# Output projection, second norm and expert search in two token halves, with one gather stream for u and v rows

## The chip, the cores and the metric

One core of a Trainium2 chip. The metric is device microseconds of one launch, the median of the runs. Engines are named as in the profile: PE is TensorE's matmuls (PEld its weight loads), DVE is VectorE, ACT ScalarE, POOL GpSimd, SP SyncE. Each engine works through its own instructions in order and waits on semaphores for the others.

## The reference, cut to what matters

One transformer layer over 512 latent tokens of width 2048, in float32:

```python
h = modulate(rms_norm(x, g_norm1), sh1, sc1)
q, k, v, bg, cg, u = split_proj(h @ w_in)          # 8 attention heads of 128, 1024 conv channels
o_attn = neighbourhood_attention(q, k, v, kc, vc, rpb)   # also sees 256 context tokens
o_conv = short_conv(u, bg, cg, w_conv)
y = concatenate([group_rms(o_attn), group_rms(o_conv)]) @ w_out
x = x + gt1 * y
h2 = modulate(rms_norm(x, g_norm2), sh2, sc2)
x = x + gt2 * peer(h2, w_pq, sub_keys, u_experts, v_experts)
```

`sh`, `sc` and `gt` come from `silu(c) @ w_ada + b_ada`, 12288 columns. `peer` chooses for each token, in each of 8 heads, 16 of 16384 experts: a query of two halves is scored against 128 keys each, the 16 best of either side are combined, and the 16 best sums win. For its 128 experts a token then computes

```python
act = gelu(einsum('nd,ned->ne', h2, u_tab[expert])) * gate
out = einsum('ne,ned->nd', act, v_tab[expert])
```

## The kernel before, in words

All activations lie transposed, features on the 128 partitions and tokens along the free axis. A weight tile is 128 x 1024 float32 (512 KB). `weights` (lines 93 to 100) loads it through a ring of four raw buffers on SP's queue, rounds it to `hi` on ACT and subtracts to `lo` on DVE, with four buffers each. Every product is then three matmuls, hi by hi, hi by lo and lo by hi (`mm3`, lines 102 to 105), so a tile of eight 128 x 128 blocks gives 24 matmuls.

The stages in order of time:

- Modulation, first half (before 136 us), then attention, one head after the other (`project`, `qk_norm`, `attention`, `out_norm`), to about 600 us.
- Convolution channels, eight groups of three projections, to 873 us. The second part of the modulation runs beside it: `ada_tasks` (line 261) is a generator, and each step loads one tile of `w_ada` through the same raw ring and multiplies and adds it on DVE (lines 293 and 295). A chunk of 1024 columns takes 16 steps, then `row_sums` and `columns_of` collect it through PE. Six of the eight chunks lie here, twelve steps a group, and two in the output projection.
- Output projection (lines 443 to 462): 16 output parts `m`, each 2 weight tiles and 48 matmuls of 512 tokens, evicted by DVE into `R` with gate and residual, stored to `x1d`, squared and summed.
- Second norm (lines 464 to 478): `rstd_of`, then for each of 16 feature blocks three operations on DVE and one on ACT that write the normalised tokens to `HH` and `HL` as hi and lo.
- Query and search (lines 533 to 650): 16 queries of 48 matmuls of 512 tokens. `half_top` takes the 16 best of 128 scores for each of four blocks of 128 tokens on DVE, `head_top` combines two of them; POOL and ACT then find the experts' numbers (lines 595, 603 to 605), and `hit_sums` reduces them on DVE. A step's parts are put one or two queries later, so that other work lies between. Six u blocks run beside the last head.
- u stage: 128 `u_block`s (line 515), each 2 weight tiles and 48 matmuls, for the first 352 tokens against all experts; gelu on ACT, stored to `gu`. Beside it `one_hots` and `scatter` build each token's gate values per expert by small matmuls and store them to `gd`.
- v stage (lines 846 to 882): 16 groups `g` of 8 column steps `dq`, each 2 weight tiles and 48 matmuls of 352 tokens. `prepare` loads a group's share of `gd` and `gu`, multiplies and splits them one group ahead; DVE adds the results into `acc`, and `finish` writes the output in the last group.

The last 160 tokens (`NG`) are not multiplied with all experts. Their rows are gathered: `gather` (line 715) issues an indirect DMA on POOL's queue that brings one row of 2048 per partition (1 MB), 160 of them from `u` and 160 from `v`, with two row buffers. A u row is multiplied with h2 and summed on DVE (line 737), a v row is scaled and added on DVE (line 745), and a buffer's next fetch goes out when its use is over. The two streams are spread by `paced`: 161 steps over the 121 u blocks that follow the search, and 161 steps over the first 120 column steps of v.

The framework plans each engine's order at build time from the program's order and its own costs; `issue_after` pins an instruction behind another (the gather's uses behind the latest weight split).

## Time and profile before

| | us |
|---|---|
| median of 3 runs | 3448.43 |
| lowest and highest | 3443.44, 3456.69 |
| the profiled execution | 3443.56 |
| its span | 3441.8 |

In the span PE is busy 3287.1 us (96%), PEld 3019.0, DVE 2492.6, ACT 1177.3 and POOL 670.8. The DMA engines moved 912.52 MB, 265 GB/s on the mean. Matmuls are pipelined: the duration of one is longer than the distance to the next, and so a busy share of 96% is not yet PE at its peak. What a matmul costs is read from the distance of two starts. A wait counts only where PE stands behind it in the end.

### The profile page before, as it was taken

The page shows a single profiled execution, that of the slowest core. Times are in us where ns is not written, and L with a number is a line of the kernel's source. Part 1 is how long each engine was busy: PE and PEld are TensorE (multiplying, and loading weights), DVE is VectorE, ACT ScalarE, POOL GpSimd, SP SyncE. Part 2 cuts the span into 40 slices and gives each one's busy share as a digit, 9 for nine tenths or more (in the row PEclk, how much of TensorE's full clock was granted, in tenths as well). Part 3 has the DMA queues.
Part 4 walks back from the last instruction along what each step waited for, and adds up shares of the span by engine and source line. Part 5 has one row for each costly group of instructions (what it writes and reads, how often), then busy time and mean ns, then how long its engine had stood idle before and what let it go on. Part 6 is the DMA issues. An engine that isn't in the chain of part 4 may idle for free.

```text
span 3441.8 us, 48157 instructions
## 1 busy us (share of the span) xinstructions
PE 3287.1 (96%) x18951; PEld 3019.0 (88%) x18951; DVE 2492.6 (72%) x3648; ACT 1177.3 (34%) x1582; POOL 670.8 (19%) x402
## 2 busy tenths in 40 slices
PE   5899999999999988999999999999989989989999
PEld 1488888878887878999999999999989989989999
DVE  4444444888756888787888887676787887878885
ACT  3344444222324454333333333333222222322222
POOL 0000000000001663222211222222323223322320
PEclk9999999999999999999999999999999999999999
DMA  8722222888772226999999999998898998989986
GB/s 303 234 67 63 66 66 61 289 278 286 242 237 85 86 83 229 334 341 336 339 343 337 328 339 340 355 360 303 319 344 316 343 343 322 353 328 336 338 323 210
DMA packets 265316, 912.52 MB, mean 265 GB/s; under 512 B 23809, under 2 KB 77313, under 8 KB 222721
## 3 DMA queue, kind: packets, MB, share of 16 engines
q1 hardware_dynamic: 208208, 527.74, 44.6%
q0 software_dynamic: 46080, 335.56, 25.7%
q10 hardware_dynamic: 10800, 46.14, 3.4%
q8 instruction: 149, 2.44, 0.3%
q14 instruction: 79, 0.64, 0.1%
HBM read 854.82 MB, written 54.53 MB: 264 GB/s over the span
## 4 chain that ended last, share of the span: by engine, by line
PE 63%; DMA 19%; DVE 10%; issue 4%; POOL 2%; ACT 1%; SPq 0%; DVEq 0%; ACTq 0%; POOLq 0%
DMA row<-v,exi 11%; PE sps L105 8%; PE sps L103 8%; PE sps L104 8%; PE xps L103 4%; PE xps L105 4%; PE xps L104 4%; DVE accg L745 3%; DMA raw<-wada 3%; DVE wlo L99 3%; PE ops L105 3%; PE ops L103 2%; PE ops L104 2%; DMA row<-u,exi 2%; PE gps L709 2%
## 5 line engine op out<-in xcount | busy, mean ns | idle before, releaser
L98 ACT ACTIVATE whi<-raw 128x1024 fp32r<-128x1024 f32 x672 | 709.2, 1058 | 1642.6 <-PE sps L104 442.1
L99 DVE TENSOR_TENSOR wlo<-raw,whi 128x1024 fp32r<-128x1024 f32 x664 | 810.2, 1237 | 283.4 <-ACT whi L98 253.6
L105 PE MATMUL sps<-HH,wlo 128*128 128x352 f32 x2048 | 665.4, 325 | 21.4 <-DVE wlo L99 21.4
L103 PE MATMUL sps<-HH,whi 128*128 128x352 f32 x2048 | 671.8, 328 | 1.1 <-ACT whi L98 1.1
L104 PE MATMUL sps<-HL,whi 128*128 128x352 f32 x2048 | 663.7, 324 | 0.0
L105 PE MATMUL ops<-Ah,wlo 128*128 128x352 f32 x1536 | 505.4, 330 | 54.1 <-DVE wlo L99 54.0
L103 PE MATMUL ops<-Ah,whi 128*128 128x352 f32 x1536 | 503.2, 328 | 5.6 <-DVE acc L877 5.6
L104 PE MATMUL ops<-Al,whi 128*128 128x352 f32 x1536 | 499.5, 325 | 0.0
L745 DVE SCALAR_TENSOR_TENSOR accg<-row,dots,accg 128x2048 f32<-128x2048 f32 x160 | 375.6, 2348 | 160.1 <-DMA row<-v,exi 160.1
L723 POOL DMA_INDIRECT row<-v,exi x160 | 300.5, 1878 | 697.0 <-DVE accg L745 672.6
L105 PEld LDWEIGHTS sps<-HH,wlo 128*128 128x128 f32 x2048 | 387.9, 189 | 24.3 <-DVE wlo L99 24.3
L103 PEld LDWEIGHTS sps<-HH,whi 128*128 128x128 f32 x2048 | 388.3, 190 | 1.4 <-ACT whi L98 1.4
L104 PEld LDWEIGHTS sps<-HL,whi 128*128 128x128 f32 x2048 | 388.3, 190 | 0.0
L723 POOL DMA_INDIRECT row<-u,exi x160 | 226.1, 1413 | 785.1 <-DVE row L737 690.8
L105 PEld LDWEIGHTS ops<-Ah,wlo 128*128 128x128 f32 x1536 | 295.5, 192 | 61.1 <-DVE wlo L99 61.1
L737 DVE SCALAR_TENSOR_TENSOR row<-row,h2row 128x2048 f32<-128x2048 f32 x128 | 291.5, 2287 | 64.9 <-DMA row<-u,exi 64.7
L103 PE MATMUL xps<-HH,whi 128*128 128x512 f32 x768 | 306.0, 398 | 2.0 <-ACT whi L98 2.0
L105 PE MATMUL xps<-HH,wlo 128*128 128x512 f32 x768 | 303.6, 395 | 0.5 <-DVE wlo L99 0.5
L104 PE MATMUL xps<-HL,whi 128*128 128x512 f32 x768 | 303.2, 395 | 0.0
L103 PEld LDWEIGHTS ops<-Ah,whi 128*128 128x128 f32 x1536 | 293.9, 191 | 6.9 <-issue 4.1
L104 PEld LDWEIGHTS ops<-Al,whi 128*128 128x128 f32 x1536 | 294.7, 192 | 0.0
L99 POOL TENSOR_TENSOR wlo<-raw,whi 128x1024 fp32r<-128x1024 f32 x8 | 20.0, 2496 | 1003.4 <-ACT whi L98 1003.4
(274 smaller groups left out, 4943.0 us busy)
## 6 DMA issues: line engine op xcount, KB each, us to landing
raw<-uT SPq DMA_DIRECT2D x256, 512.0 KB
raw<-vb SPq DMA_DIRECT2D x256, 512.0 KB
raw<-wada SPq DMA_DIRECT2D x192, 512.0 KB
raw<-win SPq DMA_DIRECT2D x96, 512.0 KB
gu<-ug ACTq DMA_DIRECT2D x64, 352.0 KB
gd<-stg ACTq DMA_DIRECT2D x11, 2048.0 KB
gt<-gd SPq DMA_DIRECT2D x32, 704.0 KB
gl<-gu SPq DMA_DIRECT2D x32, 704.0 KB
```

What stands on the lines that cost most here:

```text
L98: weights.hi = nc.scalar.activation(hi, raw, AF.Copy)
L99: weights.lo = (eng or nc.vector).tensor_tensor(lo, raw, hi.bitcast(F32), op=ALU.subtract)
L103: nc.tensor.matmul(ps, lw[0], rw[0], start=start, stop=False)
L104: nc.tensor.matmul(ps, lw[0], rw[1], start=False, stop=False)
L105: return nc.tensor.matmul(ps, lw[1], rw[0], start=False, stop=stop)
L709: nc.tensor.matmul(gps[:, j, :], oj[:, j, :], oi[:, j, :], start=True, stop=True)
L723: nc.gpsimd.indirect_dma_start(out=row.rearrange("p k d -> p (k d)"), out_offset=None, in_=ap[tab], in_offset=bass.IndirectOffsetOnAxis(ap ...
L737: nc.vector.scalar_tensor_tensor(row, row, 1.0, h2row if s < P else h2ext, op0=ALU.mult, op1=ALU.mult, accum_out=dots[:, s:s + 1])
L745: nc.vector.scalar_tensor_tensor(ag, row, dots[:, s:s + 1], ag, op0=ALU.mult, op1=ALU.add)
```

## The change

The modulation sums move: four of the eight chunks go into the attention heads (4, 5 and 5 steps after the three projections of a head, their sums in `R`'s free tiles), the other four into the convolution (9 steps a group where there were 12). None is left in the output projection.

The output projection, the second norm and the search are done for tokens 256 to 511 first, then for tokens 0 to 255. Weights of `w_out` and `w_pq` are loaded and split for each half, and their matmuls have 256 columns instead of 512. The order is: output parts of the second half; two parts of the first half; norm of the second half; search of the second half with the other fourteen output parts of the first half between its queries (`between_a`), the norm of the first half at its query 14, and five u blocks at its end; `gathered`; search of the first half with 42 u blocks between its queries (`between_b`); the other 81 u blocks; v. The POOL variant of the weight split in `query` goes.

The gather is one stream, 160 u rows and then 160 v rows in the same two buffers, 321 steps over 251 units: half a unit for each query of the second search, one for each u block after the first five and for each of the 120 column steps. The v accumulators are `h2row` and `h2ext` themselves, written first by a scaling, so the two zeroed tiles and their memsets go. The scatter's generator now takes two steps at every fourth u block. Pools change sides, and PSUM banks are dealt anew.

```diff
-BANKS = {... "query": (0, 1, 2), ... "gps": (0, 1, 2), "tp": (3,), "u": (4, 5, 6), ...
+H = T // 2
+TL = 2
+BANKS = {... "query": (2, 5), ... "gps": (0, 2, 5), "tp": (3,), "u": (4, 6, 1), ...
...
+        tasks = ada_tasks(range(4), lambda c: R[:, 4 + 2 * (c % 2):6 + 2 * (c % 2), :].rearrange("p a t -> p (a t)"),
+                          iter((r_tile(3, "rows"), r_tile(5, "rows"))).__next__)
         for hd in range(NH):
             qps, _ = project(3 * hd, False)
+            run_tasks(tasks, 4)
...
             kps, kcps = project(3 * hd + 1, True)
+            run_tasks(tasks, 5)
...
             vps, vcps = project(3 * hd + 2, True)
+            run_tasks(tasks, 5)
...
-        tasks = ada_tasks(cnv, range(0, 6))
+        tasks = ada_tasks(range(4, 8), lambda c: cnv.tile([P, 1024], F32, tag="ada", bufs=2, name="ada"),
+                          lambda: cnv.tile([P, 512], F32, tag="rows", name="rows"))
...
-            run_tasks(tasks, 4)
+            run_tasks(tasks, 3)
...
+    def out_part(m, half):
+        cols = slice(H * half, H * half + H)
+        xm = op.tile([P, H], F32, tag="xm", bufs=4, name="xm")
+        nc.sync.dma_start(xm, ap["xT"][:, m, cols])
+        ps = psum("proj", "yps", P, H)
+        for hf in range(2):
+            w = weights(ap["wout"][m, hf])
+            for k in range(8):
+                kk = 8 * hf + k
+                mm3(ps, (w[0][:, k, :], w[1][:, k, :]), (y2[kk][0][:, cols], y2[kk][1][:, cols]), kk == 0, kk == KD - 1)
+        return m, half, ps, xm
+
+    def out_evict(m, half, ps, xm):
+        cols = slice(H * half, H * half + H)
+        xo = X[:, m, :]
+        nc.vector.scalar_tensor_tensor(xo, ps, mod2[:, m:m + 1], xm, op0=ALU.mult, op1=ALU.add)
+        nc.sync.dma_start(x1d[m][:, cols], xo)
...
+    for m in range(KD):
+        out_evict(*out_part(m, 1))
...
+    early = [out_part(m, 0) for m in range(2)]
+    norm2(1)
...
-    def query(c):
-        ps = psum("query", "qps", P, T)
+    def query(c, half):
+        cols = slice(H * half, H * half + H)
+        ps = psum("query", "qps", P, H)
         for hf in range(2):
-            w = weights(ap["wpq"][c, hf], nc.gpsimd if c % 2 == 1 and hf == 0 else None)
+            w = weights(ap["wpq"][c, hf])
...
+    def search(half, qs, between):
...
+        for c in range(1, 2 * NH + 4):
+            nxt = None
+            if c < 2 * NH:
+                nxt = query(c, half)
+            between(c)
...
+    def gather():
+        rows = []
+        todo = [("u", s) for s in range(NS)] + [("v", s) for s in range(NS)]
...
+        for n, (tab, s) in enumerate(todo):
+            with tc.issue_after(mark["dve"].ins):
+                (use_u if tab == "u" else use_v)(s, rows[n])
+            fetch()
+            yield
...
+    def use_v(s, row):
+        ag = accg[0 if s < P else 1]
+        if s in (0, P):
+            nc.vector.tensor_scalar(ag, row, dots[:, s:s + 1], None, op0=ALU.mult)
         else:
+            nc.vector.scalar_tensor_tensor(ag, row, dots[:, s:s + 1], ag, op0=ALU.mult, op1=ALU.add)
...
+    def between_a(c):
+        if c <= 12:
+            out_evict(*out_part(c + 1, 0))
+        elif c == 13:
+            for m in (14, 15):
+                out_evict(*out_part(m, 0))
+        elif c == 14:
+            norm2(0)
+            ops_.close()
+            u_block.pool = us.enter_context(pool("uo", side="right", **reuse))
+        elif c >= 16:
             u_block()
+            if c == 17:
+                u_block()
+
+    qs = query(0, 1)
+    gather_rows()
+    for x in early:
+        out_evict(*x)
+    us = ExitStack()
+    search(1, qs, between_a)
...
+    gathered()
+    accg = [h2row, h2ext]
+    NGV = NGRP // 2
+    gat = paced(gather(), 2 * NS + 1, NH + 128 - u_block.n + 8 * (NGV - 1))
+
+    def between_b(c):
+        if c < 2 * NH:
+            gat(0.5)
+        for _ in range(2 + c % 2 if c < 2 * NH else 1):
+            u_block()
+            gat()
+
+    qs = query(0, 0)
+    gat(0.5)
+    search(0, qs, between_b)
...
-            for _ in range(1):
+            for _ in range(2 if n % 4 == 0 else 1):
...
-    accg = [vl.tile([P, KD, P], F32, name=f"accg{i}") for i in range(2)]
-    for x in accg:
-        nc.gpsimd.memset(x, 0.0)
...
-    gat_v = paced(gather("v", vl, use_v), NS + 1, 8 * (NGV - 1))
...
-            gat_v()
+            gat()
```

## Rows read from the trace of the kernel before

**Rows 1.** Page, the chain that ended last: shares of the span by line

```profile
DMA row<-v,exi 11%; PE sps L105 8%; PE sps L103 8%; PE sps L104 8%; PE xps L103 4%; PE xps L105 4%; PE xps L104 4%; DVE accg L745 3%; DMA raw<-wada 3%; DVE wlo L99 3%; PE ops L105 3%; PE ops L103 2%; PE ops L104 2%; DMA row<-u,exi 2%; PE gps L709 2%
```

**Rows 2.** Stretch, us, busy (count) PE, PEld, DVE, ACT, POOL; PEclk, DMA share, GB/s

```profile
136.00:600.00 464.00, 462.55 (x2651) 391.96 (x2651) 218.06 (x403) 201.82 (x364) 0.00 (x0) 1.00 0.22 67
600.00:873.00 273.00, 270.37 (x1185) 218.18 (x1184) 227.11 (x264) 87.82 (x113) 0.00 (x0) 0.99 0.82 276
...
1102.00:1260.00 158.00, 155.41 (x727) 129.62 (x726) 139.52 (x714) 73.30 (x95) 94.01 (x50) 0.99 0.27 82
1265.00:1330.00 65.00, 48.77 (x264) 47.03 (x262) 60.18 (x228) 31.22 (x42) 34.54 (x20) 0.88 0.27 86
1330.00:2130.00 800.00, 800.00 (x5225) 799.72 (x5225) 647.89 (x926) 279.13 (x402) 173.10 (x127) 1.00 0.91 336
...
2363.00:3363.00 1000.00, 940.29 (x5713) 932.07 (x5712) 800.24 (x620) 294.70 (x281) 302.72 (x162) 0.97 0.90 333
```

**Rows 3.** Gathered rows: count, ns min/median/max, first and last start us, shapes

```profile
L723 POOL DMA_INDIRECT row<-u,exi x160: 932/1147/3162, 1328.4 to 2334.4; - x160
...
L745 DVE SCALAR_TENSOR_TENSOR accg<-row,dots,accg x160: 2337/2350/2354, 2376.8 to 3370.4; 128x2048 f32<-128x2048 f32 x160
L737 DVE SCALAR_TENSOR_TENSOR row<-row,h2row x128: 2276/2285/2295, 1338.0 to 2148.1; 128x2048 f32<-128x2048 f32 x128
...
L737 DVE SCALAR_TENSOR_TENSOR row<-row,h2ext x32: 2279/2292/2294, 2151.6 to 2344.9; 128x2048 f32<-128x2048 f32 x32
```

**Rows 4.** Chain in order of time, v stage: start us, us, what

```profile
2503.78 2.34 DVE accg L745
...
2506.38 9.53 DMA row<-v,exi
2516.00 2.36 DVE accg L745
...
2556.54 0.29 PE ops L103
```

**Rows 5.** Waits from 2363 to 3370 us: total us, times, longest us

```profile
DVE accg L745 <- DMA row<-v,exi: 160.1, 80, 5.9
```

**Rows 6.** PE in time: start us, us, what; left out: 2, 13 and 19 matmuls

```profile
145.31 0.28 PE L103 MATMUL cps<-hch,whi 128*128 128x256 f32 x1
...
145.66 0.40 PE L103 MATMUL xps<-HH,whi 128*128 128x512 f32 x1
...
899.81 0.39 PE L103 MATMUL yps<-HH,whi 128*128 128x512 f32 x1
...
902.98 0.39 PE L105 MATMUL yps<-HH,wlo 128*128 128x512 f32 x1
...
1499.79 0.32 PE L103 MATMUL sps<-HH,whi 128*128 128x352 f32 x1
...
1502.99 0.32 PE L105 MATMUL sps<-HH,wlo 128*128 128x352 f32 x1
```

**Rows 7.** VectorE in order of time at the second norm

```profile
1051.50 0.75 DVE L453 SCALAR_TENSOR_TENSOR R<-yps,mod,xm 128x512 f32<-128x512 f32 x1 [8.14 <-PE yps L105]
...
1060.08 2.08 DVE L474 SCALAR_TENSOR_TENSOR R<-R,asc,r 128x512 f32<-128x512 f32 x3
...
1084.75 0.38 DVE L488 TENSOR_REDUCE selq<-ident 128x32 f32<-128x128 f32 x1
```

**Rows 8.** GpSimd, 1102 to 1260 us: xcount | busy us, mean ns | idle before, releaser

```profile
L595 POOL TENSOR_TENSOR hit<-iota,posf 128x800 f32<-128x800 f32 x24 | 42.0, 1779 | 47.2 <-DVE posf L591 47.2
L605 POOL TENSOR_TENSOR hit<-hit,both 128x800 f32<-128x800 f32 x20 | 38.8, 1975 | 6.2 <-ACT hit L604 6.2
```

**Rows 9.** The same columns, whole span: weight split and modulation sums on VectorE

```profile
L99 DVE TENSOR_TENSOR wlo<-raw,whi 128x1024 fp32r<-128x1024 f32 x664 | 810.2, 1237 | 283.4 <-ACT whi L98 253.6 <-PE xps L105 26.5 <-issue 2.0
...
L295 DVE SCALAR_TENSOR_TENSOR ada<-raw,cond,ada 128x1024 f32<-128x1024 f32 x120 | 153.9, 1282 | 57.1 <-DMA raw<-wada 55.5
```

More of the change, by code (lines that the diff above doesn't have):

```diff
@@ L480, in build @@
-    gp = es.enter_context(pool("gp", side="right", **reuse))
+            split(ys[k][:, cols], yk[0][:, cols], yk[1][:, cols])
+            if half:
+                y2.append(yk)
+    rs_.close()
     NS = P + NX
+    gp = es.enter_context(pool("gp", **reuse))
     h2row = gp.tile([P, KD, P], F32, name="h2row")
@@ new lines, in norm2 @@
+    def norm2(half):
+        cols = slice(H * half, H * half + H)
+        sqa = out_evict.sqa
+        ss = psum("aux", "ss", P, H)
+        nc.tensor.matmul(ss, ones, sqa, start=True, stop=True)
+        r2 = op.tile([P, H], F32, name="r2")
+        rstd_of(r2, ss, D, sqa)
+        for k in range(KD):
+            hk = HH[:, k, cols], HL[:, k, cols]
+            sh = mod2[:, 16 + k:17 + k]
+            nc.vector.scalar_tensor_tensor(X[:, k, :], X[:, k, :], asc2[:, k:k + 1], r2, op0=ALU.mult, op1=ALU.mult)
+            nc.scalar.activation(hk[0], X[:, k, :], AF.Identity, bias=sh)
+            nc.vector.scalar_tensor_tensor(hk[1], X[:, k, :], sh, hk[0].bitcast(F32), op0=ALU.add, op1=ALU.subtract)
+            if half:
+                nc.vector.tensor_scalar(X[:, k, ND - H:H], X[:, k, ND - H:H], sh, None, op0=ALU.add)
@@ L494, in build, with gather_rows @@
+    def gather_rows():
+        four = rp.tile([P, KD, QX, NX], F32, tag="row", bufs=2, name="four")
+        nc.gpsimd.tensor_copy(four, X[:, :, ND - H:ND - H + NX].unsqueeze(2).to_broadcast([P, KD, QX, NX]))
+        for dst, cols in ((h2row, lambda k: X[:, k, H - P:H]), (h2ext, lambda k: four[:, k].rearrange("p q x -> p (q x)"))):
             for q4 in range(4):
@@ L568, in half_top, with head_top @@
         return tops
-    def head_top(hd, first, second):
-        both = tk.tile([P, 2, 4, NP], F32, tag="cand", bufs=2, name="both")
+    def head_top(hd, half, first, second):
+        both = tk.tile([P, 2, TL, NP], F32, tag="cand", bufs=2, name="both")
         o = 0
@@ L592, in head_top @@
         hits = []
[L593 to L594 removed]
+        for t in range(TL):
+            hit = tk.tile([P, 16, NP], F32, tag="hit", bufs=4, name="hit")
             nc.gpsimd.tensor_tensor(hit, iota[:, 0:NP].unsqueeze(1).to_broadcast([P, 16, NP]),
@@ L597, in head_top, with hit_masks @@
             hits.append(hit)
-        return hd, hits, cidx
-    def hit_masks(hd, hits, cidx):
-        for t in range(4):
+        return hd, half, hits, cidx
+    def hit_masks(hd, half, hits, cidx):
+        for t in range(TL):
             with tc.issue_after(gate["act"].ins):
@@ new lines, in paced, with step @@
+    def paced(gen, steps, units):
+        state = [0, 0]
+        def step(weight=1.0):
+            state[0] += weight
+            want = min(steps, int(-(-state[0] * steps // units)))
+            while state[1] < want:
+                state[1] += 1
+                run_tasks(gen, 1)
+        step.state = state
+        return step
+    def between_a(c):
[9 more added lines that the diff above has]
+        elif c >= 16:
+            u_block()
+            if c == 17:
+                u_block()
@@ L713, in scatter @@
             nc.scalar.dma_start(gd[tok // CH], scatter.stg)
-    def gather(tab, rp, use):
-        rows = []
-        def fetch():
-            s = len(rows)
-            if s == NS:
-                return
-            row = rp.tile([P, KD, P], F32, tag="row", bufs=2, name="row")
-            nc.gpsimd.indirect_dma_start(out=row.rearrange("p k d -> p (k d)"), out_offset=None, in_=ap[tab],
-                                         in_offset=bass.IndirectOffsetOnAxis(ap=exi[:, s:s + 1], axis=0))
-            rows.append(row)
-        fetch()
-        fetch()
-        yield
-        for s in range(NS):
-            with tc.issue_after(mark["dve"].ins):
-                use(s, rows[s])
-            fetch()
-            yield
-    def use_u(s, row):
-        nc.vector.scalar_tensor_tensor(row, row, 1.0, h2row if s < P else h2ext, op0=ALU.mult, op1=ALU.mult, accum_out=dots[:, s:s + 1])
-        if s % 4 == 3:
-            sl = slice(s - 3, s + 1)
-            nc.scalar.activation(dots[:, sl], dots[:, sl], AF.Gelu)
-            nc.vector.tensor_tensor(dots[:, sl], dots[:, sl], gtg[:, sl], op=ALU.mult)
-    def use_v(s, row):
-        ag = accg[0 if s < P else 1]
-        nc.vector.scalar_tensor_tensor(ag, row, dots[:, s:s + 1], ag, op0=ALU.mult, op1=ALU.add)
-    def paced(gen, steps, units):
-        state = [0, 0]
-        def step():
-            state[0] += 1
-            want = min(steps, -(-state[0] * steps // units))
-            while state[1] < want:
-                state[1] += 1
-                run_tasks(gen, 1)
-        return step
-    gathered()
     hots = one_hots()
     ready, built = [], []
-    gat_u = None
     vs = ExitStack()
```

237 lines of the change are left out of this document (105 added, 132 removed).

## The prediction

> **What bounds it now.** Read first the chain of waits by line: beside the matmuls its longest item is the landing of rows gathered from the v table, 11% [rows 1]. Then the busy time by stretch [rows 2]: from 136 to 873 us and from 1330 to 2130 us TensorE (PE) has matmuls in flight nearly all the time (800.00 of 800), so there the kernel costs what its matmuls cost. It falls short in two places. Between 1265 and 1330 us it is busy 48.77 of 65 us at a granted clock of 0.88, while VectorE (DVE) is at 60.18: the search's last head holds up the u blocks. And from 2363 to 3363 us it is busy 940.29 of 1000 at 0.97.
>
> What ends last in that v stretch? The rows' own views tell [rows 3, 4]. From 2376.8 to 3370.4 us there are 160 uses, 159 steps of 6.25 us. A buffer's cycle is a use (2.34 us), an issue gap and a landing (9.53 us), 12.2 us from use to use; with two buffers that is 6.1 us a row. DVE works in order, so a late row holds up the weight split behind it: 160.1 us of such waits, 80 times [rows 5]. Matmuls after a stall are 0.29 us apart in the chain [rows 4] where 0.16 is usual, so a stall costs more than its length. PE's own pace: 352 columns take (1502.99 - 1499.79)/20 = 0.160 us [rows 6], so a unit of 48 (one u block, or one column step dq of a v group) takes 7.68 us. The v gather does 161 steps in 120 units, 1.342 a unit, so a unit takes 1.342 x 6.25 = 8.39 us: 0.71 x 120 = 85 us are lost to rows. In the u stretch the 128 first rows come every (2148.1 - 1338.0)/127 = 6.38 us without harm; once the scatter matmuls are gone the units shrink and the last 32 come every (2344.9 - 2151.6)/31 = 6.24 us. So 6.25 us is what two buffers give when pressed.
>
> **The change, part by part.**
>
> *Narrow matmuls.* Output projection and query each turn 768 matmuls of 512 columns into 1536 of 256. Rows: 512 columns (902.98 - 899.81)/14 = 0.226 us, 256 columns (145.66 - 145.31)/3 = 0.117 us [rows 6]. A pair costs 0.007 us more; times 1536, **+11 us** (0 to 21 by the rounding of the rows), all on PE's path.
>
> *Weights read and split twice.* 64 more tiles of 512 KB and 64 more splits. In the output half a part is 48 x 0.117 = 5.6 us of PE for two tiles, 2 x 1.24 us of DVE [rows 9] and an eviction: hidden under PE. In-order queues remain: the x1 store sits on SP's (SyncE's) queue between weight loads and waits for the eviction, and the prefetch, still eight tiles deep, now covers half the time. **+4** (0 to 15).
>
> *Modulation sums moved.* Four of eight chunks, 64 tiles of 1.28 us DVE each [rows 9] and 33.5 MB, go into the attention stage, where DVE is at 218 of 464 us and DMA at 0.22 [rows 2]. Room is ample, but the tiles share four raw buffers with the weights and stand in DVE's in-order queue ahead of the softmax and the query/key norm, which PE waits for. The convolution carried twelve such tiles per group at 227 of 273 DVE and PE still had 270.37 of 273 [rows 2], so I take **+8** (0 to +35, a tenth of their 82 us to under a half). Convolution and output projection get lighter: **-3** (-8 to 0).
>
> *Second norm and first search.* From the last eviction (1051.50) to the first row fetch (1328.4) are 277 us [rows 3, 7]. The work in it is 768 x 0.226 + 6 u blocks x 7.68 + about 192 small matmuls at 0.11 = 241 (the 0.11 is an estimate, the 256-column spacing rounded down): 36 lost. After, by halves: rstd chain 8.6 us, now some 6.5; sixteen rounds of normalising took 24.7 us [rows 7], some 17 at half width; two early output parts and the first query cover 17 of the 24, so 7 lost. The second norm has only two queries (11.3) beside 20 us of its own and 6 of the search's DVE work: some 13 lost. The last head's chain has half the operations: 13 for 26. A round of search beside an output part needs of DVE 4 tiles x 1.24, 0.9 for the eviction and its sum, and the search of two token blocks. That search: 139.52 us of DVE over some 13.5 queries (158 us at 11.7 of PE each) is 10.3, less 2.0 for tiles is 8.3, halved 4.4 with what doesn't shrink. Together 10.3 of 11.7 us of PE, 88%; today's stage has DVE at 88% and PE at 155.41 of 158 [rows 2], so 3 lost. Sum 36: **0** (-15 to +25).
>
> *Second search beside the gather.* A round is one query and 2.5 u blocks: 5.6 + 19.2 + 0.4 = 25.2 us of PE. DVE: 7 tiles x 1.24 [rows 9], 3.84 rows x 2.29 [rows 3], 4.4 of search: 21.9, 87%. At 81% PE loses nothing (1330 to 2130), at 88% some 1.6% [rows 2]; rows that wait add to it. **+12** over 15 rounds (3 to 35).
>
> *One stream.* 321 steps over 8 + 123 + 120 = 251 units are 1.279 a unit, before 1.33 (u) and 1.342 (v). Its start needs nothing new: the accumulators take the rows of h2 when u is done, so the two memsets go. At 6.25 us a row a v unit takes 7.99 us: 0.40 x 120 = **-48**. Ends: if not the row cycle but the bytes bind, a unit moves 2.75 MB instead of 2.82 (rows, two weight tiles, the coefficients' share), 8.39 becomes 8.19: -24; if rows keep up, 7.68: -85. I take the row-cycle value, since the last u rows, beside other traffic, show the same 6.24. In the u stage the 23 units without scatter lost 0.6 us each; now the scatter ends six units before v: **-12** (-14 to 0). But the first v coefficients now have some seven units for load, product and split where they had twelve, the load waits on SP's queue for the last scatter store, and weight loads stand behind it: **+5** (0 to 15).
>
> A rule speaks for the far end. The Trainium skill (DMA: Bandwidth & Descriptors, "Anatomy of one DMA — SWDGE (gpsimd) path") fits about 2.0 us plus bytes over 436 GB/s. By it a 1 MB row would land in 4.4 us, an estimate from that page, and v would run at PE's pace, -85 in place of -48. Here the landing was 9.53 us [rows 4], with weights and a second row in the air, and the measurement decides.
>
> **Sum.** +11 +4 +8 -3 +0 +12 -48 -12 +5 = -23. From the profiled execution (3443.6 us, its span 3441.8) that is 3421. That execution lies at the low end of the runs (3443.4 to 3456.7, median 3448.4), so against the median it is nearer -0.8% than -0.7%.
>
> **The rivals.**
>
> *The bytes bind in v.* For it: DMA is busy 0.90 there at 333 GB/s [rows 2]. Against: 336 GB/s at 0.91 did no harm from 1330 to 2130. Then v gives 24 and the late u units little: 3421 + 24 + 9 = 3454, no change.
>
> *Rows keep up.* Stalls also drop the clock (0.97), so fewer may vanish together. Then v gives 85: 3421 - 37 - 4 = 3380.
>
> *Slower: GpSimd's (POOL's) queue in the second search.* Row fetches now share POOL with the search's hit operations, and a hit operation waits for DVE with the next fetch behind it. Per head: 2 x 1.78 + 2 x 1.98 = 7.5 us of work and 47.2/6 = 7.9 us of waiting for four blocks, 3.9 for two [rows 8]. The stream has little to give: 7.7 rows per head at a paced 6.6 us against 6.25 leave 2.7 us. So the rows fall behind 7.5 + 3.9 - 2.7 = 8.7 us per head, DVE waits for them in order, and eight heads make 70 where I counted 12: 3479. It decides once fetches stand behind hit operations by more than those 2.7 us a head. Against it: an issue takes 0.93 to 3.16 us [rows 3], four split tiles give PE 15 us of cover, and the planner may set the hits between fetches. The Trainium skill (SBUF — State Buffer, "Who interferes with whom") adds a lock: a DVE operation on the shared port pair keeps GpSimd out until it ends, descriptor writing too. The spread of the issue times agrees with that without proving it.
>
> *The moved sums get in attention's way*: 35 where I took 8: 3448, no change.
>
> **How the numbers follow.** Forecast 0.44 (its own range 3400 to 3440), bytes bind 0.17, rows keep up 0.14, POOL's queue 0.16, attention 0.09. The time is the forecast's, 3421. The range 3375 to 3482 reaches from just under "rows keep up" to just over "POOL's queue". About 0.5% is what a measurement of this kernel can tell from no change; it lies at 3426 and 3461. Faster: 0.31 of the forecast's 0.44, all of "rows keep up", 0.01 else: 0.46. Slower: POOL's queue 0.16 and the upper ends of two others 0.04: 0.20. Same: 0.34.
>
> **What would show it.** Uses of v rows still 6.2 to 6.3 us apart with units near 8.0: the row cycle. Uses 6.0 apart and a clock of 1.00: rows keep up. Uses 6.4 or more with DVE waiting for v rows: bytes. In the second search, DVE waits for u rows of over 2 us a row and fetches right behind hit operations: the slower rival. Attention's stage should grow by under 10 us, the output halves should run at 0.117 us a matmul. The prediction is wrong at its root if PE has long gaps at the two norms, or if the stream reaches v later than the u blocks do.

## The result, and the profile after

The changed kernel takes 3466.25 us (median; the kernel before, in the same runs, 3445.68): a ratio of 1.0058, 95% interval 1.0046 to 1.0071. The forecast was 3421, faster; it is slower by just over the half per cent that can be told from no change. The profiled execution has a span of 3467.7 us against 3441.8. All splits below are made between these two spans, +25.9 us where the sum said -23. They are good to some 6 us: the changed kernel and five of those below, with the same code up to the output projection, reach its first matmul between 887.9 and 893.5 us.

The chain that ended last, shares of the span by line, still has the v rows in it, with less than the 11% of [rows 1]:

```profile
PE sps L107 8%; PE sps L106 8%; PE sps L105 8%; DMA row<-v,exi 7%; PE ops L107 5%; PE ops L105 4%; PE ops L106 4%; PE gps L815 2%; DVE wlo L101 2%; PE yps L106 2%; PE yps L105 2%; PE yps L107 2%; PE hps L105 1%; PE hps L106 1%; PE hps L107 1%
```

Stretches of the changed kernel, columns as in [rows 2]: attention, convolution, the norm of tokens 256 to 511 (1000), the end of their search with the norm of tokens 0 to 255 (1186), second search (1248) and its tail (1648), u blocks (1710), v (2420):

```profile
136.00:620.00 484.00, 475.30 (x2695) 397.73 (x2695) 294.69 (x473) 208.30 (x374) 0.00 (x0) 0.99 0.44 139
620.00:890.00 270.00, 270.00 (x1167) 215.36 (x1166) 184.82 (x236) 85.99 (x122) 0.00 (x0) 1.00 0.65 211
...
1000.00:1035.00 35.00, 27.91 (x187) 25.13 (x186) 29.04 (x77) 19.88 (x38) 1.89 (x1) 0.90 0.35 110
...
1186.00:1248.00 62.00, 46.36 (x290) 44.26 (x290) 60.14 (x189) 36.77 (x58) 20.41 (x12) 0.89 0.37 118
1248.00:1648.00 400.00, 395.15 (x2711) 393.90 (x2710) 340.58 (x674) 159.49 (x221) 166.92 (x87) 1.00 0.85 317
1648.00:1710.00 62.00, 54.17 (x311) 52.89 (x310) 53.01 (x113) 22.49 (x32) 22.34 (x14) 0.92 0.72 263
1710.00:2348.00 638.00, 637.96 (x4127) 637.39 (x4126) 522.04 (x799) 224.05 (x326) 138.44 (x92) 1.00 0.88 327
2420.00:3400.00 980.00, 938.64 (x5752) 932.93 (x5752) 792.30 (x622) 297.17 (x284) 304.46 (x151) 0.98 0.89 336
```

The uses of v rows, columns as in [rows 3]; the last starts at 3396.5 us:

```profile
L707 DVE SCALAR_TENSOR_TENSOR h2row<-row,dots,h2row x127: 2341/2350/2355, 2364.5 to 3195.4; 128x2048 f32<-128x2048 f32 x127
...
L707 DVE SCALAR_TENSOR_TENSOR h2ext<-row,dots,h2ext x31: 2345/2351/2354, 3206.6 to 3396.5; 128x2048 f32<-128x2048 f32 x31
```

DVE's waits for v rows in the same stretch (us, times, longest), which [rows 5] answers to with 160.1:

```profile
DVE h2row L707 <- DMA row<-v,exi: 108.8, 58, 5.1
DVE h2ext L707 <- DMA row<-v,exi: 28.4, 18, 3.1
```

Two milestones cut the kernel in three: the first matmul of the output projection and the last evicted u block, which come at 874.4 and 2364.0 us before. Each row gives the stretch since the row above it.

| until | before | after | measured | predicted |
|---|---|---|---|---|
| first output matmul | 874.4 | 891.1 | +16.7 | +8 - 3 = +5 |
| last u eviction | 2364.0 | 2420.2 | +39.5 | +11 +4 +0 +12 -12 +5 = +20 |
| end of span | 3441.8 | 3467.7 | -30.3 | -48 |

All three parts missed, by 12, 20 and 18 us, all in the same direction. The eviction is ACT's, and it starts 0.8 us behind the end of the last u matmul before and 4.4 us after; counted from PE's first v matmul (2363.0 and 2415.7 us) the last two rows are +36.0 and -26.8. DVE's queue carried the gather through the second search with little harm (PE busy 395.15 of 400 us), and the v stage did gain. So neither of the two rivals "POOL's queue" and "bytes bind" explains the sign by itself. One thing that the trace shows and no term of the sum has is this: the spacing of like matmuls changed. In the u stage of the kernel before, 352 columns take an even 0.160 us [rows 6]. In the changed one they take 0.158 during the second search, then (but for a few blocks at its end) 0.167 from 1737 to 1938 us, 0.158 to 2164 us, and 0.167 to about 2390. PE in time, the second of these turns; each pair of rows around it spans 46 steps of a u block, and the three transposes of a one-hot group stand between:

```profile
1928.33 0.33 PE L106 MATMUL sps<-HL,whi 128*128 128x352 f32 x1
...
1935.99 0.33 PE L107 MATMUL sps<-HH,wlo 128*128 128x352 f32 x1
...
1938.05 0.27 PE L790 MATMUL ijtp<-ident,ij 128*128 128x128 f32 x1
1938.16 0.27 PE L791 MATMUL ijtp<-ident,best 128*128 128x128 f32 x1
...
1938.43 0.32 PE L106 MATMUL sps<-HL,whi 128*128 128x352 f32 x1
...
1945.72 0.32 PE L107 MATMUL sps<-HH,wlo 128*128 128x352 f32 x1
```

7.66/46 = 0.1665 us ahead of the transposes, 7.29/46 = 0.1585 behind them, at a granted clock of 1.00 on both sides, by the same lines of code. Some 430 us at 0.167 in place of 0.160 are 18 us lost, some 620 us at 0.158 are 6 gained: about 12 us net.

### The profile page after: what moved, and what is told of

It is laid out like the page before. It is cut to its first block, busy times and chain, and to the rows that moved or that the text cites. A ratio compares the mean times of both kernels' runs of the same rounds, so it can differ in the third digit from the quotient of the medians.

```text
span 3467.7 us, 51890 instructions
## 1 busy us (share of the span) xinstructions
PE 3314.5 (96%) x20489; PEld 3103.4 (89%) x20489; DVE 2609.9 (75%) x3898; ACT 1255.6 (36%) x1735; POOL 721.3 (21%) x392
## 4 chain that ended last, share of the span: by engine, by line
PE 54%; DMA 9%; DVE 7%; issue 2%; POOL 0%; ACT 0%; DVEq 0%; SPq 0%; ACTq 0%; POOLq 0%
PE sps L107 8%; PE sps L106 8%; PE sps L105 8%; DMA row<-v,exi 7%; PE ops L107 5%; PE ops L105 4%; PE ops L106 4%; PE gps L815 2%; DVE wlo L101 2%; PE yps L106 2%; PE yps L105 2%; PE yps L107 2%; PE hps L105 1%; PE hps L106 1%; PE hps L107 1%
## 5 line engine op out<-in xcount | busy, mean ns | idle before, releaser
L100 ACT ACTIVATE whi<-raw 128x1024 fp32r<-128x1024 f32 x736 | 776.4, 1058 | 1557.3 <-PE sps L106 403.2
L101 DVE TENSOR_TENSOR wlo<-raw,whi 128x1024 fp32r<-128x1024 f32 x736 | 907.2, 1249 | 249.6 <-ACT whi L100 231.0
L682 POOL DMA_INDIRECT row<-v,exi x160 | 319.0, 1994 | 726.4 <-DVE h2row L707 573.5
L682 POOL DMA_INDIRECT row<-u,exi x160 | 255.3, 1595 | 755.7 <-DVE row L696 569.9
L707 DVE SCALAR_TENSOR_TENSOR h2row<-row,dots,h2row 128x2048 f32<-128x2048 f32 x127 | 298.3, 2349 | 112.6 <-DMA row<-v,exi 112.5
L696 DVE SCALAR_TENSOR_TENSOR row<-row,h2row 128x2048 f32<-128x2048 f32 x128 | 305.5, 2390 | 78.4 <-DMA row<-u,exi 78.0
```

The source lines that it names most:

```text
L100: weights.hi = nc.scalar.activation(hi, raw, AF.Copy)
L101: weights.lo = (eng or nc.vector).tensor_tensor(lo, raw, hi.bitcast(F32), op=ALU.subtract)
L682: nc.gpsimd.indirect_dma_start(out=row.rearrange("p k d -> p (k d)"), out_offset=None, in_=ap[tab], in_offset=bass.IndirectOffsetOnAxis(ap ...
L696: nc.vector.scalar_tensor_tensor(row, row, 1.0, h2row if s < P else h2ext, op0=ALU.mult, op1=ALU.mult, accum_out=dots[:, s:s + 1])
L707: nc.vector.scalar_tensor_tensor(ag, row, dots[:, s:s + 1], ag, op0=ALU.mult, op1=ALU.add)
```

## The experiments

**The moved sums alone.** In the kernel before, the changed kernel's edits for the modulation sums (4, 5 and 5 steps a head in attention, 3, 3 and 3 a group in the convolution):

```diff
+        tasks = ada_tasks(range(4), lambda c: R[:, 4 + 2 * (c % 2):6 + 2 * (c % 2), :].rearrange("p a t -> p (a t)"),
+                          iter((r_tile(3, "rows"), r_tile(5, "rows"))).__next__)
...
-        tasks = ada_tasks(cnv, range(0, 6))
+        tasks = ada_tasks(range(4, 8), lambda c: cnv.tile([P, 1024], F32, tag="ada", bufs=2, name="ada"),
+                          lambda: cnv.tile([P, 512], F32, tag="rows", name="rows"))
...
-        tasks = ada_tasks(op, range(6, 8))
```

> The kernel before with one part of the change alone: the modulation sums moved (chunks 0 to 3 into the attention stage, 4 to 7 into the convolution, none left in the output projection). Moved-sums theory: the first matmul of the output projection comes some 17 us later than in the kernel before, as in the changed kernel (874.4 there, 890.9 here), and the time grows by 15 to 18 us less what a lighter output projection gives (0 to 3): +12 to +18 us. Rival (the 17 us belong to the half-wise weights and their prefetch, not to the sums): first matmul within 4 us of 874.4, time within 5 us of the kernel before.

Measured: 3449.12 us, ratio 1.0015 (0.9997 to 1.0032). First output matmul, count, ns, first and last start:

```profile
L103 PE MATMUL yps<-HH,whi x256: 388/389/398, 882.4 to 1056.8; 128*128 128x512 f32 x128
```

882.4 is +8.0, half of the 17, and by the last u block only 1.1 us of it are left (2365.1 against 2364.0). The result fell between the two answers: the sums cost the start 8 us, as predicted, and the end almost nothing. The other half of the 17 had to come from something else.

**The spacing: an odd number of matmuls?** The turns stand where three transposes run, an odd number. So first a fourth:

```diff
             nc.tensor.transpose(tp[:, 2, :], bt, ident)
+            nc.tensor.transpose(tp[:, 3, :], bt, ident)
```

> The changed kernel with a fourth transpose, which nobody reads, beside the three of each one-hot group, so that each group adds an even number of matmul instructions to PE's queue. Parity theory: the 352-column spacing stays at 0.158 us through the whole u stage instead of 0.167 in its first and last thirds; about 50 blocks x 48 x 0.0083 = 20 us less. Rival (the spacing has nothing to do with the number of instructions; it follows the traffic or the scatter): the thirds stay as they are and the time stays within 5 us.

Measured: 3480.58 us, ratio 1.0085 (1.0059 to 1.0110): 14 slower, where 20 faster was expected. The trace says why. PE in time of this kernel around its second group, four transposes now:

```profile
1937.32 0.27 PE L791 MATMUL ijtp<-ident,best 128*128 128x128 f32 x1
1937.42 0.27 PE L792 MATMUL ijtp<-ident,best 128*128 128x128 f32 x1
...
1937.70 0.32 PE L106 MATMUL sps<-HL,whi 128*128 128x352 f32 x1
...
1945.36 0.33 PE L107 MATMUL sps<-HH,wlo 128*128 128x352 f32 x1
```

7.66/46 = 0.1665: no turn, here or at the third group, as the theory has it. But the spacing went to 0.167 at 1736 us, behind a run of eight scatter matmuls and no transpose, and stayed there to the end of the stage. Eight is even, so the count alone is not the rule. Of the ten times nine lie from 3476 to 3486 us and one at 3445, so not every execution need have gone this way; only one was profiled. One more transpose, in the middle of the first group:

```diff
                 x = (P * t + t0) % 16
+                if t == 0 and q == 5:
+                    with tc.issue_after(mark["pe"].ins):
+                        nc.tensor.transpose(tp[:, 3, :], bt, ident)
```

> The changed kernel with four transposes in each one-hot group, and one more, unread, in the middle of the first group: one odd insertion after the slow spacing has begun at about 1737 us. Parity theory: spacing 0.167 us from about 1737 us to the inserted transpose (some 25 to 50 us), 0.158 from there to the end of the u stage; against the kernel with four transposes alone (0.167 to the end, 3480 us) some 31 us less, 3449 us; against the changed kernel some 17 us less. Rival (the spacing follows the traffic or the place of the tiles): 0.167 to the end, 3480 us.

Measured: 3466.86 us, ratio 1.0057 (1.0018 to 1.0097), its four times spread from 3447 to 3477. In the profiled one (3458.1) the extra transpose came to stand exactly at 1735 us, where the kernel with four transposes turns to 0.167; here it did not turn, and 0.158 held to the end. Its last u eviction is at 2407.5 us, that of the kernel with 0.167 to the end at 2430.9: the two spacings are worth 23 us over this stage. The run can't tell whether the odd transpose undid a turn or no turn came: the eight scatter matmuls that turned the other kernel stand right ahead of it. Nor does its 3467 us, between the two answers, decide.

Counted over the nine profiled kernels that have the two spacings, the changed one and those below among them, the spacing turned at 16 of 18 groups of three transposes (12 of 12 second and third groups), at 2 of 9 groups of four (0 of 6), and at 9 of some 640 runs of eight or sixteen scatter matmuls. So it is a lasting condition that an odd insertion nearly always turns over and an even one seldom does. What starts it stays open.

**The convolution.** Its 512-column matmuls show the same thing, 0.2325 us after and 0.227 before (means of some 1100 neighbouring starts; the expectations put the second at 0.2275).

```diff
+            if g == 2:
+                one = psum("aux", "sums", P, 512)
+                nc.tensor.transpose(one[:, 0:P], ident, ident)
```

> The changed kernel with one unread transpose put between two projections of the third convolution group. The 512-column matmuls of the convolution stand 0.2325 us apart in the changed kernel and 0.2275 in the one before, though nothing in their code differs. If a lasting state of the PE queue sets this, and an odd insertion turns it over: 0.2325 until the transpose, 0.227 behind it, the output projection begins some 4 us earlier (886 to 887 us); whether the state reaches the u stage is open. Rival (the place of the tiles in memory, which the change moved): 0.2325 throughout, output projection at 891 us.

Measured: 3464.57 us, ratio 1.0059 (1.0029 to 1.0088); 0.2325 us ahead of the transpose and behind it, first output matmul at 893.4. The rival holds in this execution: here one insertion turns nothing.

**The place in memory.** The change moves its pools: the tiles of the inputs, of the projections' operands and of the halves of h lie at the other end of the on-chip memory. This can be done alone. In the kernel before, every working pool changes ends, in the changed one every pool changes back, with no instruction added or reordered (in the traces PE's stages, and every instruction of DVE, ACT and POOL, come in the same order); the constants and the weight ring stay:

```diff
-    hp = hs.enter_context(pool("hp"))
+    hp = hs.enter_context(pool("hp", side="right"))
-    big = rs_.enter_context(pool("big"))
+    big = rs_.enter_context(pool("big", side="right"))
-    with pool("cnv", side="right", **reuse) as cnv:
+    with pool("cnv", **reuse) as cnv:
...
```

> The kernel before with every working pool moved to the other end of the on-chip memory (the pools of inputs and halves of h to the right end, as the changed kernel has them, the others to the left end); no instruction is added, removed or reordered. Place theory: the spacing of the matmuls hangs on where their operands lie. The convolution's 512-column matmuls go from 0.2275 to 0.2325 us (1180 of them, +6 us at the first matmul of the output projection, 874.4 to about 880), and the u stage shows the two spacings 0.158 and 0.167 of the changed kernel in place of its even 0.160. Rival (it hangs on the order of instructions, which is the same here): 0.2275 and 0.160, time within 4 us of the kernel before.

> The changed kernel with its working pools mirrored back (inputs and halves of h at the left end, as in the kernel before); no other change. Place theory: 0.2275 us in the convolution and 0.160 throughout the u stage; the convolution gives back 6 us, the u stage about 10: some 3450 us. Rival: 0.2325 and the two spacings 0.158 and 0.167 stay, time within 5 us of the changed kernel's 3466.

Measured: the kernel before with its pools mirrored 3462.72 us, ratio 1.0059 (1.0042 to 1.0076), as slow as the change. The changed kernel with its pools put back 3452.24 us, ratio 1.0028 (1.0014 to 1.0041), 14 faster than it was. PE in the convolution, 640 to 840 us: us, busy and matmuls, clock, DMA share, GB/s. The changed kernel, and then the one with its pools put back:

```profile
640.00:840.00 200.00, 200.00 (x863) 1.00 0.72 235
```

```profile
640.00:840.00 200.00, 200.00 (x883) 1.00 0.70 231
```

The kernel before and its mirrored form:

```profile
640.00:840.00 200.00, 197.37 (x866) 0.99 0.85 284
```

```profile
640.00:840.00 200.00, 200.00 (x866) 1.00 0.84 282
```

With the pools put back PE does 20 matmuls more in 200 us. In the kernel before, though, both forms do 866: there PE idled 2.63 us in the stretch beside more traffic. That the slower spacing fills this gap would explain part of why its first output matmul stayed at 874.1 where I expected 880; it is argued, and 6 us is what two executions can differ by there. Its u stage shows the two spacings of the changed kernel; here the turn at its second one-hot group:

```profile
1629.60 0.33 PE L104 MATMUL sps<-HL,whi 128*128 128x352 f32 x1
...
1637.27 0.33 PE L105 MATMUL sps<-HH,wlo 128*128 128x352 f32 x1
...
1638.54 0.27 PE L685 MATMUL ijtp<-ident,best 128*128 128x128 f32 x1
...
1638.82 0.32 PE L104 MATMUL sps<-HL,whi 128*128 128x352 f32 x1
...
1646.10 0.32 PE L105 MATMUL sps<-HH,wlo 128*128 128x352 f32 x1
```

7.67/46 = 0.1667, then 7.28/46 = 0.1583. The changed kernel with its pools put back has 0.160 throughout, by 50 us bins 0.1600 to 0.1607; here 46 steps ahead of its second group and 46 behind it:

```profile
1915.98 0.32 PE L106 MATMUL sps<-HL,whi 128*128 128x352 f32 x1
...
1923.34 0.32 PE L107 MATMUL sps<-HH,wlo 128*128 128x352 f32 x1
...
1925.78 0.32 PE L106 MATMUL sps<-HL,whi 128*128 128x352 f32 x1
...
1933.19 0.32 PE L107 MATMUL sps<-HH,wlo 128*128 128x352 f32 x1
```

7.36/46 = 0.1600 and 7.41/46 = 0.1611. So the place alone decides whether the two spacings exist; what turns one into the other is above. Every profiled kernel agrees: the five with `hp` and `big` at the left end have 0.227 and 0.160, the nine with them at the right end the others. The four kernels here also narrow it down for the convolution. Its own pool `cnv` lies right in the kernel before and in the changed one and left in both mirrored ones, so it doesn't decide; the weight ring never moved; what is left are `hp`, which holds `HH` and `HL`, the matmuls' moving operand, and `big`, which holds `R`. Which of the two, and why a place does this, stays open. The PSUM banks and the order of instructions are out, since the mirrored kernels leave them as they were.

**The v rows.** A third buffer for v rows alone, in the kernel before and in the changed one (there in space that opens as v begins):

```diff
-            row = rp.tile([P, KD, P], F32, tag="row", bufs=2, name="row")
+            row = rp.tile([P, KD, P], F32, tag="row", bufs=3 if tab == "v" else 2, name="row")
```

```diff
-            row = rp.tile([P, KD, P], F32, tag="row", bufs=2, name="row")
+            if third and n % 3 == 0:
+                row = third[0].tile([P, KD, P], F32, tag="row3", name="row")
+            else:
+                row = rp.tile([P, KD, P], F32, tag="row", bufs=2, name="row")
...
+            if third and not third[1]:
+                third[1] = True
+                fetch()
...
+    third += [vl, False]
```

> The kernel before with three row buffers in place of two for the v gather alone. Row-cycle theory (a buffer's use, issue and landing set 6.25 us a row): a third buffer lets rows come every 4 us if asked, PE's own pace decides, a v unit falls from 8.39 us to 7.7 to 7.8, DVE's 160 us of waits for v rows go, and the time falls by 70 to 85 us. Bytes theory (the queues together can't bring more than some 336 GB/s): the landing grows with the third row in flight, a unit stays at 8.2 to 8.39 us and the time falls by 0 to 24 us.

> The changed kernel with a third row buffer for the v gather, taken in the space that opens when the u stage is done. Row-cycle theory (in the one stream too, a unit with two rows waits for a buffer's cycle): a v unit falls from 8.14 us to PE's 7.65, as in the kernel before with three buffers; 0.49 x 120 = 59 us less, some 3407 us. Rival (what is left above PE's pace in the changed v stage comes from bytes or from VectorE's longer queue, not from buffers): under 20 us less, the landing grows with the third row in flight.

Measured: 3353.84 us, ratio 0.9734 (0.9707 to 0.9761), and 3409.74 us, ratio 0.9901 (0.9879 to 0.9924): 94 and 57 us gained, by far the largest effects in this study. The v stage of the kernel before with three buffers, then its uses of rows and DVE's wait for them:

```profile
2363.00:3270.00 907.00, 905.39 (x5682) 904.15 (x5681) 797.67 (x621) 292.43 (x278) 324.68 (x159) 1.00 0.96 368
```

```profile
L745 DVE SCALAR_TENSOR_TENSOR accg<-row,dots,accg x160: 2344/2347/2384, 2370.3 to 3275.2; 128x2048 f32<-128x2048 f32 x160
```

```profile
DVE accg L745 <- DMA row<-v,exi: 3.3, 2, 3.0
```

Waits fall from 160.1 to 3.3 us, the clock from 0.97 rises to 1.00, and the queues carry 368 GB/s where 333 looked like a limit [rows 2]. From the last u eviction (2357.5) to the last use are 917.7 us, 7.65 a unit, PE's own pace. The changed kernel with three:

```profile
2430.00:3340.00 910.00, 906.13 (x5684) 904.87 (x5683) 784.76 (x616) 294.65 (x280) 303.15 (x149) 1.00 0.93 358
```

(3343.1 - 2426.2)/120 = 7.64 us a unit. The row cycle was right, the bytes were not, in both kernels. The landing itself did not shrink (median 9.5 us with three rows in the air, of the 20 landings that the profile of the kernel before holds; 9.1 with two in the changed kernel); the third buffer hides it. The Trainium skill (DMA: Bandwidth & Descriptors, "Anatomy of one DMA — SWDGE (gpsimd) path"), by whose fit for one DMA I estimated 4.4 us, does not agree with this trace: beside the other traffic a row takes more than twice that to land, and v runs at PE's pace all the same.

The same question from the other side, fewer v rows for each unit:

```diff
-    gat = paced(gather(), 2 * NS + 1, NH + 128 - u_block.n + 8 * (NGV - 1))
+    UW = 1.09
+    gat = paced(gather(), 2 * NS + 1, UW * (NH + 128 - u_block.n) + 8 * (NGV - 1))
```

> The changed kernel with its gather stream shifted by weight: a u unit counts 1.09 instead of 1, so u units take 1.33 rows and v units 1.22 instead of 1.279 each. Row-cycle theory: a v unit is 1.22 x 6.36 = 7.77 us in place of 8.14, 120 of them -45 us, against some +5 in the u stage. Bytes theory: a v unit moves 0.057 MB less of 2.75, 2%: -19 us at most, and as much back in the u stage if it were bound by bytes too.

Measured: 3430.01 us, ratio 0.9945 (0.9929 to 0.9961), 36 less than the changed kernel and faster than before. Its last uses:

```profile
L707 DVE SCALAR_TENSOR_TENSOR h2ext<-row,dots,h2ext x31: 2344/2350/2355, 3168.7 to 3360.3; 128x2048 f32<-128x2048 f32 x31
```

(3360.3 - 2419.1)/120 = 7.84 us a unit, where the row cycle said 7.77 and the bytes 7.98. The u stage did not suffer (last eviction 2419.1 for 2420.2).

**The sums put back.** In the changed kernel, none in attention, six chunks in the convolution (4 steps in place of 3, three times a group), two in the first output half:

```diff
-        tasks = ada_tasks(range(4), lambda c: R[:, 4 + 2 * (c % 2):6 + 2 * (c % 2), :].rearrange("p a t -> p (a t)"),
-                          iter((r_tile(3, "rows"), r_tile(5, "rows"))).__next__)
...
-        tasks = ada_tasks(range(4, 8), lambda c: cnv.tile([P, 1024], F32, tag="ada", bufs=2, name="ada"),
+        tasks = ada_tasks(range(6), lambda c: cnv.tile([P, 1024], F32, tag="ada", bufs=2, name="ada"),
...
+    tasks = ada_tasks(range(6, 8), lambda c: X[:, 12:16, :].rearrange("p a t -> p (a t)") if c == 6 else op.tile([P, 1024], F32, name="ada"),
+                      lambda: op.tile([P, 512], F32, name="rows"))
     for m in range(KD):
         out_evict(*out_part(m, 1))
+        run_tasks(tasks, 3)
```

> The changed kernel with one part undone: the modulation sums go back where they were (chunks 0 to 5 in the convolution, 6 and 7 beside the first output half), none in the attention stage. Moved-sums theory: attention gets its 13 us back, the convolution takes 5 more, the first matmul of the output projection comes at 882 to 884 us in place of 890.9; the first output half, with 32 sums of 1.28 us beside 90 us of matmuls at DVE 88%, loses 3 to 6 us of it; the time falls by 2 to 6 us. Rival (the sums cost nothing that lasts, as in the kernel before with them moved, whose time didn't change): first matmul some 8 us earlier and the time within 3 us, because the output half loses all of it.

Measured: 3504.31 us, ratio 1.0172 (1.0155 to 1.0189), 38 slower than the changed kernel. The first output matmul came at 877.1, 14 us earlier, and the first output half then lost all of it and 37 more: the first query starts at 1043.0, 165.9 us later, where the changed kernel needs 114.5 (891.1 to 1005.6). Neither answer had this. SP's queue from 880 to 1040 us, in this kernel and then from 895 to 1000 in the changed one:

```profile
SPq L487 <- DVE X L486: 50.1, 16, 5.8
```

```profile
SPq L492 <- DVE X L491: 11.1, 15, 1.1
```

The x1 store waits on SP for an eviction that stands in DVE's queue behind three sum tiles, and the weight loads stand behind the store. ACT waits for the same evictions before it squares them, with the rounding of weights behind that in its queue, and PE waits longest for the rounding (this kernel, 880 to 1040 us):

```profile
ACT sq L493 <- DVE X L486: 59.4, 9, 9.5
PE yps L105 <- ACT whi L100: 26.6, 9, 10.5
```

So two in-order queues stand behind the laden DVE in a half that is 51 us longer. I priced SP's at 4 us, in the changed kernel, where it has little to do. How much of the 51 is SP's and how much ACT's was not tried. Moving the sums out of the halves was needed for halves of this size.

**Both causes together.** First the changed kernel's third buffer with the even and odd transposes, then the same buffer with the pools put back; all are edits shown above.

> The changed kernel with the third v row buffer and with the even transposes and the one odd insertion together. If the two causes are independent their gains add: -59 and -17 us, some 3390 us, which is faster than the kernel before by 1.6%. If the faster u stage runs into its rows (6.36 us a row at 1.279 a unit is 8.1 us, above PE's 7.6), the second gain is under 8 us: some 3400 us.

> The changed kernel with the pools mirrored back and a third row buffer in the v gather: both causes taken out of the changed kernel at once. If they are independent: 3452 - 56 = 3396 us; what is then left above the kernel before with a third row buffer (3354 us), some 42 us, is the price of the token halves and the moved sums, since rows hold up neither. Rival (the third buffer's gain belongs in part to the place of the tiles): over 3406 us.

Measured: 3411.66 us, ratio 0.9904 (0.9864 to 0.9944), from 3396 to 3427, no better than the third buffer alone. In the profiled one (3420.3) the spacing turned to 0.167 at 1798 us, at a scatter, and the even groups never turned it back. With the pools put back 3393.13 us, ratio 0.9861 (0.9837 to 0.9885), where the sum of the two said 3396: within the intervals the causes are independent. What remains above the kernel before with three buffers, 3393 - 3354 = 39 us (44 by the two ratios, give or take 12), is what the token halves, the moved sums and the rest of the change cost once neither rows nor place blur it. That kernel, at 3354 us, is the best of all here: before, with one more buffer.

## Why the prediction was wrong

Three steps failed: a cost that is not in the sum, the size of its one large gain, and the price of the narrow matmuls.

**The step that failed first is one that is not in it.** The pools that change ends were costed at nothing, without a word. They are worth 14 us of the 45 between forecast and result (3466.25 to 3452.24; 10 by the ratios 1.0058 and 1.0028, each against its own runs of the kernel before). Between the two profiled spans it is 22.7 us: 10.5 up to the first output matmul, of which the convolution's spacing explains some 6 (1167 matmuls at 0.005), 5.3 up to the last u block, and 6.9 in v, for which I saw no cause and which two executions can differ by. Without them the change is at +0.28%, which by the bound set above is no change: they decided that it came out slower, not that it brought no gain.

With the pools put back, the milestones are 880.6, 2404.4 and 3445.0 us: +6.2, +34.2 and -37.2 against the kernel before (+28.8 and -31.8 if counted by PE's first v matmul, at 2398.0). The steps stand against these.

**Moved sums: right.** +5 forecast, +6.2 measured. In attention DVE now works 294.69 us of 484, with [rows 2] at 218.06 of 464, and PE idles 8.7 us where it idled 1.45. The rival (35) is out.

**Narrow matmuls: mis-sized.** I read 0.117 us from four matmuls in attention. Over the first output half:

```profile
894.42 0.27 PE L105 MATMUL yps<-HH,whi 128*128 128x256 f32 x1
...
899.27 0.28 PE L105 MATMUL yps<-HH,whi 128*128 128x256 f32 x1
```

4.85 us for 40 steps, 0.121; the mean of 808 neighbouring starts from 890 to 1005 us is 0.1199, and with the pools put back 0.1201. A pair costs 2 x 0.120 - 0.227 = 0.013 us more than one wide matmul, times 1536 is 20 us, not 11. The upper bound of 21 held it.

**Norms and searches: right in size.** By counted matmuls times their spacing, the kernel before loses 37 us from the output projection to the first row fetch (36 forecast). The changed one loses some 55 to the end of the second search: +18 where +4, 0 and +12 were forecast. Some 10 of them fall in the first output half (114.5 us for 867 matmuls of 0.120), where weights read twice had been given 4. Most of the rest is where PE waits, mainly for DVE: 7.1 us of PE idle at the norm of tokens 256 to 511 (4.2 of them for ACT), 15.6 at the end of the first search, 7.8 at the second's tail.

**POOL's queue: out.** DVE waited 38.6 us for u rows in the second search, 17 times, but PE idled 4.85 of 400 us there: the weight tiles already split covered it, as the counter-argument had it.

**Late u units: wrong by half of a small term.** Forecast -12 and +5. The kernel before lost 9.5 us in its last 233 us of u, not 14, and the changed one loses 6.5 in its last 70. PE waits there 4.2 us for DVE's weight split, three times; that late v coefficients cause it, as forecast, is not shown.

**One stream: the gain came, at two thirds of its size.** A v unit takes (3396.5 - 2420.2)/120 = 8.14 us, 8.08 with the pools put back, not 7.99: -30 or -37 for -48. Counted from PE's first v matmul it is 8.17 and 8.13, -27 or -32. The step that failed is the constant: 6.25 us a row times rows per unit, for every unit alike. Measured at three rates, a unit takes 8.39, 8.14 and 7.84 us at 1.342, 1.279 and 1.222 rows, so a row costs 6.25, 6.36 and 6.42 us, and one row less per unit gives back 4.0 to 5.2 us, not 6.25. The traces show why one constant doesn't fit: the rows do not slow every unit, they stop a few. Take each of the 120 units from its first matmul to the first of the next. In the kernel before 94 of them take at most 7.75 us, PE's own pace, and the other 26 hold the loss, 86 us above 7.65 a unit, up to 17 us for one; 53 us of it lie at the seventh of a group's eight column steps. In the changed kernel 19 units hold 62 us, with fewer v rows a unit 8 hold 28, and in the kernel before with three buffers 4 hold 2.5. PE's waits in v, 2363 to 3370 us before and 2416 to 3396 after, are for weight splits, which stand in DVE's queue behind the late rows:

```profile
PE ops L105 <- DVE wlo L99: 54.0, 22, 6.1
```

```profile
PE ops L107 <- DVE wlo L101: 39.1, 16, 6.1
```

That the tiles already split cover a late row until they are used up fits this, and is argued; why the seventh step runs out most often stays open. By the prediction's own signs 6.36 us a row lies between the row cycle (6.2 to 6.3) and the bytes (6.4 or more); it was the third buffer that told them apart.

Sum of the misses with the pools put back: sums 1, narrow 9, norms and searches 2, late u 4, v 11, together 27, where 26 lie between the forecast's -23 and this kernel's +3.2 (3445.0 - 3441.8). The place adds the other 22.7. With milestones good to some 6 us, so close a sum is in part luck.

**The bounds.** That the range (3375 to 3482) held the time was luck: several small misses of one direction add up to about what one rival was given, for a cause that did not come. What no rival had is the combination that came: the narrow matmuls near their upper bound, the one gain at some two thirds, and a cost outside the list. And "rows keep up", which I gave 0.14, was right about what rows are worth (85 us; the third buffer took 88.5 off the v stage, 1077.8 to 989.3): only the change didn't buy it. The prediction's own row, two buffers and 12.2 us from use to use [rows 3, 4], said that a third buffer would.

## What to carry to other kernels

Where a cycle of buffer, issue and landing binds, another buffer is worth more than a better pace: here 8 KB a partition gave 94 us, and one stream for the rows 30 in the same stage, which the rest of the change took back. Before splitting a stage for cover, price the doubled instruction count by a long run of like matmuls, not by a few. A move of tiles in memory is an edit too: mirror the pools alone, once, and read the spacing of like matmuls in both.

## What was not expected of the hardware

TensorE's spacing of like matmuls depends on where tiles lie in the on-chip memory, at a granted clock of 1.00: in the convolution 512 columns 0.227 or 0.2325 us, in the u stage 352 columns an even 0.160 us in one place and 0.158 or 0.167 in the other. Not everywhere: in attention 512 columns stand 0.232 us apart on the mean in both places, and 256 columns 0.120 in the output halves. In the other place the spacing lasts for hundreds of us and mostly turns at odd insertions (three transposes in 16 of 18 groups; four in 2 of 9). The two spacings are 23 us apart over a 700 us stage. One kernel's own four times spread by 30 us (3447 to 3477); that the spacing does this is not shown, with one profile each. The Trainium skill (SBUF — State Buffer, "Who interferes with whom") has it that TensorE never waits on another engine for a port; these traces don't show a port, but they show that TensorE's pace is not a constant of the matmul's shape. What sets the first spacing of an execution, and which tile does it, was not tried.
